# A two-layer diffusion trunk: attention recorded one block ahead, the differential maps combined on GpSimd, new durations in the order planner, a mask padded to 128 rows

## The chip, the cores and the metric

The kernel runs on one core of one Trainium2 chip. The metric is the device time of one execution in microseconds. Before the change the median of three runs is 3346.67 us (3345.6 to 3353.66).

## What is computed

Two layers of a transformer-like trunk over 1024 latent tokens and 256 context tokens of width 1024. Each layer normalises and modulates its input, projects it with one wide matrix, and gives the columns to four head groups: a state-space scan (SSD), grouped-query attention, a gated linear recurrence, and differential attention. Their outputs are concatenated, projected and added to the stream; a squared-ReLU MLP of width 4096 follows. Latent tokens attend to context and latent tokens (1280 keys), context tokens to context alone (256 keys), and the context stream is not needed after the second layer's attention.

The change concerns the two attentions. In the reference they are:

```python
def block_attention(q, k, v):
...
        s = jnp.einsum('bqgrd,bkgd->bgrqk', qblk, k, preferred_element_type=jnp.float32) * scale
        pr = jax.nn.softmax(s, axis=-1).astype(v.dtype)
        return jnp.einsum('bgrqk,bkgv->bqgrv', pr, v)
...
def diff_attention(q, k, v, lam, lam_init, subln_g):
    o1 = block_attention(q[:, :, 0::2], k[:, :, 0::2], v)
    o2 = block_attention(q[:, :, 1::2], k[:, :, 1::2], v)
    o = (o1.astype(jnp.float32) - lam * o2.astype(jnp.float32))
    o = rms_norm(o, subln_g) * (1.0 - lam_init)
```

So a differential head has two softmax maps over the same values. The kernel subtracts the second map, times a factor per query, from the first, and multiplies the result by the values once.

## The kernel before

**Recording and planning.** The program is written as a recording. Methods of `Trunk` call `Sched.op` for every group of instructions of one engine (matmuls that belong together are one operation), with the tiles it reads and writes and a cost in nanoseconds. Then `Sched.due` (line 380) runs along PE's operations in the order of recording, adds up their costs to due times, and carries these back through the dependences (less `HOP`, and `STRETCH` times the cost) to a priority for every operation. `Sched.run` (line 414) simulates the five queues PE, ACT, DVE, POOL and SP: an engine that is free takes the ready operation of highest priority whose new tiles can be had, and what it takes is emitted in that order. An operation that depends on another becomes ready at that one's end plus a gap: `LAT`, 150 ns, between two engines other than PE, 200 ns if either is PE. A tile's slot comes free `LAT` after its last use. On the chip every engine works through its own list strictly in that order and waits on semaphores, so the planner decides orders and slots, not times. Costs come from `act_cost` (line 290), `dve_cost` (line 299), `pool` (line 351) and `mm_cost` (line 366). An operation may be allowed on ACT or DVE (`copy("ANY", ...)`); the planner takes the one that it thinks will be done first. All instructions carry line 606, where they are emitted, so that the profile tells them apart by tile names.

**Slots.** `Trunk.__init__` (line 653) sets the classes: 30 wide SBUF tiles S with quotas per use (probability maps gP 4 and dP 8, transposed maps gT 5 and dT 5), 8 small tiles m (of which attention's statistics am may have 2), and the eight PSUM banks: scores in two groups of three banks (from 3 and from 0), transposes in 6 and 7, the value product in 6.

**A layer** (line 1628) runs its steps in the order of `ORDER`: recurrences, projections and SSD, then the attention groups G1D1 and G0D0, then the output projection in two halves, the norm and the MLP. In a group one grouped-query stream (G, two heads) and one differential stream (D, two heads of two maps) go side by side. Layer 0 has 10 query blocks of 128 (the last two are context blocks with 256 keys), layer 1 has 8.

**A block of a stream** is `att_block` (line 1399). Queries are loaded from DRAM for four G blocks or two D blocks at once (tile qt). For each of 2 or 4 maps: score matmuls (ks, qt; 12 per block and stream) into a PSUM tile of 1280 columns; one DVE instruction that scales them by the query's norm into P and takes the minimum for each row; one ACT exponential with the sum for each row. In a D block DVE then takes reciprocals, forms the factor per row (tile am), and combines the two maps of each head with one three-operand instruction over 1280 columns. After that come 20 transposes, four to a PSUM bank, copied to the tiles PT by ACT or DVE. Every second block multiplies the transposed maps of two blocks by the values (PT, V: 20 matmuls with 64-column weights, two instructions each) into one bank, in two operations. Every four blocks `attn_out` (line 1488) brings in the row factors (fac; in a D stream a norm as well, with a power on POOL, tiles asq and om) and stores the result. `attention` (line 1522) calls `att_block` for G and then D, block after block, so a block is recorded whole, up to the value product, before the next.

**The SSD mask.** `ssd_dt` (line 1156) writes cumulated sums as two groups of 10 rows, at rows 0 and 32, into a zeroed tile R of 42 rows; `ssd_group` (line 1190) spreads one of its rows over all partitions with a matmul against `pick`, also of 42 rows, 36 times in all.

Of the kernel before, what the change touches and what calls it, by code (L numbers as in the profile page):

```python
# [13 lines left out]
ALU = mybir.AluOpType  # L14
# [141 lines left out]
class Sched:  # L156
    LAT = 150.0
    HOP = 220.0
# [140 lines left out]
    def dve_cost(self, method, fast=False, n=None, **kw):  # L299
# [114 lines left out]
    def run(self, trace=None):  # L414
# [31 lines left out]
        table = 0  # L446
        done = 0
# [39 lines left out]
        while done < n:  # L487
# [9 lines left out]
            for e in names:  # L497
# [29 lines left out]
                progress = True  # L527
                if e == "ACT":
# [37 lines left out]
                for tl in o.tiles:  # L566
                    tl.ops_left -= 1
                    tl.end = max(tl.end, end)
                    if tl.ops_left == 0 and tl.slot is not None:
                        heapq.heappush(releases, (tl.end + self.LAT, tl.cls, tl if tl.cls == "psum" else tl.slot, tl.stream))  # L570
# [77 lines left out]
class Trunk:  # L648
# [27 lines left out]
    def setup(self):  # L676
# [7 lines left out]
        self.pick = self.const(10, "pick", dt=F32R)[0:42, :]  # L684
        s.copy("DVE", self.pick, c[0:42, 438:448])
# [470 lines left out]
    def ssd_dt(self, l, dtraw):  # L1156
# [21 lines left out]
        s.op("POOL", [("memset", dict(ap=R[0:42, 0:1024].f, constant=0.0))], 1300)  # L1178
# [11 lines left out]
    def ssd_group(self, l, g, xs, B, C, zmake):  # L1190
# [37 lines left out]
        for i, c in enumerate(order):  # L1228
# [6 lines left out]
            s.mms([dict(out=pb.v, lhsT=self.pick[:, c:c + 1].bc([42, 128]), rhs=self.acr[0:42, 512 * g:512 * g + 512],  # L1235
# [538 lines left out]
```

## Time and profile before

| | |
|---|---|
| median of the runs shown | 3346.67 us |
| the runs | 3346.67, 3353.66, 3345.6 us |
| profiled execution, first to last instruction | 3352.2 us |
| instructions | 45841 |
| mean granted TensorE clock | 0.990 |
| busy: PE, PEld, DVE, ACT, POOL | 97%, 78%, 65%, 35%, 4% |

The profiled execution has no other time of its own than this span. PE is TensorE's matmuls, PEld its weight loads, which run beside the matmuls; DVE is VectorE, ACT ScalarE, POOL GpSimd, SP the engine that issues the DMAs. A matmul is written as its weights' rows x columns and the moving operand's shape, so that 128*64 128x256 has weights of 64 columns. Matmuls overlap in their records, and a late one is a longer one, so that a busy PE need not be one at its full rate; spacing from start to start tells more.

### The profile page before, as it was taken

Reading aid. Unit: us, or ns where it says so; the run is one execution under the profiler, and the core shown is the slowest. Engines: PE = TensorE matmul, PEld = TensorE weight load, DVE = VectorE, ACT = ScalarE, POOL = GpSimd, SP = SyncE. Lnnn points to the kernel's source line nnn. Section 1 sums busy time; section 2 is a strip of 40 time slices with the busy share of each in tenths; the row PEclk is TensorE's granted clock in tenths of the full one; section 3 lists DMA queues with packets and bytes.
Section 4 is the critical chain, followed back from the end, with each engine's and each line's share of the span. In section 5 each row is a group of like instructions: output and inputs, shape, how many; then the busy total and the mean of one; then the engine's idle time right before and its main releaser. Section 6 shows DMA issues by size and latency. Waiting matters only on the chain. (4 is left out here: it accounts for less than half of the span.)

```text
span 3352.2 us, 45841 instructions
## 1 busy us (share of the span) xinstructions
PE 3258.6 (97%) x18456; PEld 2622.8 (78%) x18456; DVE 2171.1 (65%) x3785; ACT 1166.4 (35%) x2026; POOL 147.1 (4%) x168
## 2 busy tenths in 40 slices
PE   8999989999999999999999999999999999999999
PEld 6877786677688888887887888886677788888887
DVE  4787789894565555554556688689883655555554
ACT  5554447772311110101112554438771311111111
POOL 0010040000000000000000010030000000000000
PEclk9999999999999999999999989989999999999999
DMA  8443261416212222212110321151433111111111
GB/s 247 140 125 97 89 175 41 110 35 232 70 48 75 72 79 67 78 57 85 42 45 26 118 73 50 57 154 39 97 116 121 41 51 51 51 44 46 49 50 57
DMA packets 253868, 276.51 MB, mean 82 GB/s; under 512 B 22876, under 2 KB 212184, under 8 KB 253656
## 3 DMA queue, kind: packets, MB, share of 16 engines
q1 hardware_dynamic: 253656, 273.59, 27.0%
q8 instruction: 145, 2.38, 0.3%
q14 instruction: 67, 0.55, 0.1%
HBM read 218.75 MB, written 54.79 MB: 82 GB/s over the span
## 5 line engine op out<-in xcount | busy, mean ns | idle before, releaser
L606 DVE SCALAR_TENSOR_TENSOR hR<-banks,mod,hR 128x512 f32<-128x512 f32 x720 | 497.2, 697 | 420.4 <-PE banks L606 420.4
L606 PE MATMUL banks<-uh,wh 128*128 128x512 f32 (+1 forms) x1808 | 682.4, 377 | 5.8 <-ACT cvr L606 1.9
L606 PE MATMUL banks<-uh,wl 128*128 128x512 f32 (+1 forms) x1808 | 669.1, 370 | 1.7 <-DVE wl L606 1.7
L606 PE MATMUL banks<-ul,wh 128*128 128x512 f32 (+1 forms) x1808 | 669.0, 370 | 1.3 <-DVE ul L606 1.2
L606 ACT ACTIVATE wh<-wr 128x1024 fp32r<-128x1024 f32 (+2 forms) x193 | 189.5, 992 | 1050.7 <-PE banks L606 1009.9
L606 PE MATMUL banks<-hh,wh 128*128 128x512 f32 (+1 forms) x1280 | 476.7, 372 | 0.0
L606 PE MATMUL banks<-hl,wh 128*128 128x512 f32 (+1 forms) x1280 | 475.5, 371 | 0.0
L606 PE MATMUL banks<-hh,wl 128*128 128x512 f32 (+1 forms) x1280 | 474.8, 371 | 0.0
L606 PEld LDWEIGHTS banks<-uh,wh 128*128 128x128 f32 x1808 | 341.3, 189 | 98.8 <-issue 26.1
L606 PEld LDWEIGHTS banks<-uh,wl 128*128 128x128 f32 x1808 | 340.6, 188 | 65.4 <-DVE wl L606 3.0
L606 PEld LDWEIGHTS banks<-ul,wh 128*128 128x128 f32 x1808 | 341.1, 189 | 61.5 <-DVE ul L606 3.7
L606 DVE TENSOR_SCALAR_CACHE_REDUCE P<-banks,rq 128x1280 f32<-128x1280 f32 (+1 forms) x216 | 301.3, 1427 | 29.4 <-PE banks L606 28.1
L606 DVE TENSOR_TENSOR r<-r 128x512 f32<-128x512 f32 x160 | 102.2, 639 | 333.6 <-ACT r L606 331.4
L606 PEld LDWEIGHTS banks<-hh,wh 128*128 128x128 f32 x1280 | 240.8, 188 | 53.5 <-DVE hR L606 5.3
L606 ACT ACTIVATE P<-P,am 128x1280 f32<-128x1280 f32 (+1 forms) x216 | 273.4, 1272 | 21.1 <-DVE P L606 19.8
L606 PEld LDWEIGHTS banks<-hh,wl 128*128 128x128 f32 x1280 | 240.4, 188 | 44.7
L606 PEld LDWEIGHTS banks<-hl,wh 128*128 128x128 f32 x1280 | 240.6, 188 | 43.3
L606 PE MATMUL banks<-wh,uh 128*128 128x256 f32 (+2 forms) x784 | 250.4, 319 | 6.0 <-DVE qkw L606 4.2
L606 DVE TENSOR_TENSOR wl<-wr,wh 128x1024 fp32r<-128x1024 f32 (+2 forms) x204 | 230.4, 1137 | 27.6 <-ACT wh L606 26.1
L606 PE MATMUL banks<-ks,qt 128*128 128x512 f32 (+1 forms) x800 | 220.8, 387 | 20.2 <-DVE P L606 15.7
L606 PE MATMUL banks<-wl,uh 128*128 128x256 f32 (+2 forms) x784 | 226.3, 289 | 0.0
L606 PE MATMUL banks<-wh,ul 128*128 128x256 f32 (+2 forms) x784 | 225.5, 288 | 0.0
(241 smaller groups left out, 4341.0 us busy)
## 6 DMA issues: line engine op xcount, KB each, us to landing
wr<-in_w_mlp_dram SPq DMA_DIRECT2D x128, 512.0 KB
wm<-in_w_mod_dram SPq DMA_DIRECT2D x96, 512.0 KB
wr<-in_w_in_dram SPq DMA_DIRECT2D x40, 512.0 KB
ks<-dk SPq DMA_DIRECT2D x64, 160.0 KB
qt<-dq SPq DMA_DIRECT2D x72, 128.0 KB
wr<-in_w_out_dram SPq DMA_DIRECT2D x64, 128.0 KB
hd<-hT SPq DMA_DIRECT2D x8, 640.0 KB
ks<-gk SPq DMA_DIRECT2D x16, 320.0 KB
```

The source lines that it names most:

```text
L606: getattr(e, method)(**args)
```

## The change

The attention is split into three lists of units: `att_scores` (query load, score matmuls, scaling, exponential, and after the last map the factors and the combination), `att_turns` (transposes and copies) and `att_values` (value product and output). `attention` merges, for every block number, the score units of this block (of G and D in turn) with the transposes and values of the block before (first G's, then D's), by their weights; the transposes of D therefore stand in the second half of the next block's units.

In a D block the one combining DVE instruction per head becomes two on POOL: the second map times the factor, in place, and the first map plus this. The factor lies in am, which now is in use until the second multiplication.

The planner's numbers change: fixed parts of ACT and DVE instructions go up to about 160 to 205 ns and those of accumulating forms with them, gaps go down (35 ns between engines, 200 after PE, 55 before PE, slots free after 55, or 200 after PE), matmul costs are set anew, and an operation of PE whose weights have another tile shape than the one before is charged 190 ns. An operation on POOL with rate 1.0 is costed at 147 ns + 1 ns per element.

The SSD mask's R and `pick` get 128 rows; the rows added are zero.

```diff
-    LAT = 150.0
-    HOP = 220.0
+    LAT = 35.0
+    HOP = 150.0
+    DRAIN = 200.0
+    SWITCH = 190.0
...
-        return (52 if in_.t.cls == "psum" else 94) + n / 1.2 + 93 * aps + (93 if "accum_out" in kw else 0)
+        return (169 if in_.t.cls == "psum" else 205) + n / 1.2 + 90 * aps + (200 if "accum_out" in kw else 0)
...
+        elif method == "tensor_tensor_scan":
+            rate = 2.13
...
-        return 69 + rate * n + 61 * aps
+        return 157 + rate * n + 57 * aps + (83 if "accum_out" in kw else 0)
...
         if rhs.dt == F32R:
-            return 2.5 + (n / 2.4 if n >= 256 else n * 4 / 2.4)
-        return 2.5 + max(n * 4 / 2.4, 187)
+            return max(4 + n * 0.4453, 112)
+        return max(5 + n * 4 / 2.4, 216)
...
-        return self.op("PE", [("matmul", c) for c in calls], cost + 10)
+        return self.op("PE", [("matmul", c) for c in calls], cost)
...
+                if e == "PE":
+                    m = self.mode(o)
+                    if m != mode:
+                        mode = m
+                        o.cost += self.SWITCH
...
-                        gap = 0 if a == e and not o.nbytes else 200 if "PE" in (a, e) else self.LAT
+                        gap = 0 if a == e and not o.nbytes else self.DRAIN if e == "PE" else 55 if a == "PE" else self.LAT
...
-        self.pick = self.const(10, "pick", dt=F32R)[0:42, :]
-        s.copy("DVE", self.pick, c[0:42, 438:448])
+        self.pick = self.const(10, "pick", dt=F32R)
+        s.copy("DVE", self.pick.v, c[:, 438:448])
...
-        s.op("POOL", [("memset", dict(ap=R[0:42, 0:1024].f, constant=0.0))], 1300)
+        s.op("POOL", [("memset", dict(ap=R[:, 0:1024].f, constant=0.0))], 1300)
...
-            s.mms([dict(out=pb.v, lhsT=self.pick[:, c:c + 1].bc([42, 128]), rhs=self.acr[0:42, 512 * g:512 * g + 512],
+            s.mms([dict(out=pb.v, lhsT=self.pick[:, c:c + 1].bc([128, 128]), rhs=self.acr[:, 512 * g:512 * g + 512],
...
-                s.stt(P1[:, k0:NT], P2[:, k0:NT], m[:, 36 + h:37 + h], P1[:, k0:NT], ALU.mult, ALU.add)
+                s.pool("tensor_scalar", rate=1.0, out=P2[:, k0:NT], in0=P2[:, k0:NT], scalar1=m[:, 36 + h:37 + h],
+                       scalar2=None, op0=ALU.mult)
+                s.pool("tensor_tensor", out=P1[:, k0:NT], in0=P1[:, k0:NT], in1=P2[:, k0:NT], op=ALU.add)
```

The new `attention` and what it calls, cut to the units:

```python
    def att_scores(self, st, blk, nblk):
...
        w = sum(cn for _, cn in chunks) * (2 if gqa else 1) / 1280
        return [(w, lambda i=i: softmax(i)) for i in range(nsub)]
    def att_turns(self, st, blk):
...
        return [(0.75, lambda k=k, q=q: turn(k, q)) for k, q in keys]
    def att_values(self, st, blk, nblk):
...
        return [(3.0, lambda n=n: part(n)) for n in range(len(parts))]
    def attention(self, l, what):
...
        late = []
        for blk in range(nblk + 1):
            early = []
            if blk < nblk:
                runs = [self.att_scores(st, blk, nblk) for st in sts]
                for x in itertools.zip_longest(*runs):
                    early += [u for u in x if u]
            units = []
            for side in (early, late):
                total = sum(w for w, _ in side)
                at = 0.0
                for w, f in side:
                    units.append((at / total, len(units), f))
                    at += w
            for at, _, f in sorted(units, key=lambda u: u[:2]):
                yield (blk + at) / (nblk + 1)
                f()
            late = []
            if blk < nblk:
                for st in sts:
                    late += self.att_turns(st, blk)
                    if blk % 2:
                        late += self.att_values(st, blk, nblk)
```

## Rows read from the trace of the kernel before

**Rows 1.** The page's busy times: us, share of the span, instructions

```profile
PE 3258.6 (97%) x18456; PEld 2622.8 (78%) x18456; DVE 2171.1 (65%) x3785; ACT 1166.4 (35%) x2026; POOL 147.1 (4%) x168
```

**Rows 2.** Busy by stretch, in layer 1's MLP; columns as in rows 3

```profile
2800.00:2900.00 100.00, 100.00 (x433) 81.01 (x432) 53.78 (x72) 13.19 (x16) 0.00 (x0) 1.00 0.15 43
```

**Rows 3.** By stretch: length, PE, PEld, DVE, ACT, POOL busy us (x), clock, DMA, GB/s

```profile
488.00:770.00 282.00, 260.28 (x1890) 193.36 (x1889) 252.41 (x434) 219.16 (x391) 7.14 (x5) 0.99 0.27 76
...
1900.00:2250.00 350.00, 333.61 (x2147) 289.83 (x2147) 284.65 (x613) 169.57 (x344) 50.15 (x55) 0.95 0.27 79
2250.00:2515.00 265.00, 246.75 (x1749) 183.04 (x1748) 235.05 (x361) 202.53 (x336) 8.56 (x5) 0.99 0.30 86
```

**Rows 4.** PE's timeline in layer 0's attention: start us, length us, instructions

```profile
607.54 0.60 PE L606 MATMUL banks<-cst,P 128*128 128x128 f32 x4
...
609.95 4.54 PE L606 MATMUL banks<-PT,V 128*64 128x256 f32 x40
...
615.61 1.09 PE L606 MATMUL banks<-cst,fac 128*64 128x128 f32 x16
```

**Rows 5.** PE groups by form, 2250 to 2515: busy us, mean ns | idle before, releasers

```profile
L606 PE MATMUL banks<-cst,P 128*128 128x128 f32 x622 | 90.0, 279 | 9.2 <-ACT PT L606 6.0 <-DVE P L606 1.2 <-DVE PT L606 0.8
L606 PE MATMUL banks<-ks,qt 128*128 128x512 f32 x256 | 88.3, 436 | 8.2 <-DVE P L606 7.4
...
L606 PE MATMUL banks<-PT,V 128*64 128x256 f32 x600 | 68.9, 382 | 0.4 <-ACT PT L606 0.2
...
L606 PE MATMUL banks<-ks,qt 128*128 128x256 f32 x128 | 31.8, 297 | 0.0
```

**Rows 6.** PE groups by form, 488 to 770

```profile
L606 PE MATMUL banks<-cst,P 128*128 128x128 f32 x664 | 95.6, 278 | 8.4 <-ACT PT L606 5.0 <-DVE P L606 1.2 <-DVE PT L606 0.9
L606 PE MATMUL banks<-ks,qt 128*128 128x512 f32 x252 | 86.7, 438 | 10.6 <-DVE P L606 8.4 <-DMA qt<-dq 1.7
L606 PE MATMUL banks<-PT,V 128*64 128x256 f32 x656 | 75.2, 382 | 1.3 <-ACT PT L606 1.1
L606 PE MATMUL banks<-ks,qt 128*128 128x256 f32 x158 | 37.7, 299 | 0.1
```

**Rows 7.** DVE and ACT groups by form, 2250 to 2515

```profile
L606 DVE TENSOR_SCALAR_CACHE_REDUCE P<-banks,rq 128x1280 f32<-128x1280 f32 x96 | 145.4, 1546 | 11.5 <-PE banks L606 10.8
L606 ACT ACTIVATE P<-P,am 128x1280 f32<-128x1280 f32 x96 | 130.9, 1370 | 10.6 <-DVE P L606 10.0
...
L606 ACT ACTIVATE PT<-banks 128x512 f32<-128x512 f32 x123 | 68.7, 598 | 19.4 <-PE banks L606 16.4 <-issue 2.7
...
L606 DVE SCALAR_TENSOR_TENSOR P<-P,am,P 128x1280 f32<-128x1280 f32 x32 | 48.3, 1549 | 0.5
...
L606 ACT ACTIVATION_READ_ACCUMULATOR P<-P,am 128x1 f32 x96 | 19.5, 203 | 0.0
...
L606 DVE RECIPROCAL am<-am 128x4 f32<-128x4 f32 x16 | 2.8, 175 | 4.7 <-ACT P L606 4.7
```

**Rows 8.** POOL groups by form: the power (2250 to 2515), two memsets (whole span)

```profile
L606 POOL TENSOR_TENSOR om<-om,cst 128x8 f32<-128x8 f32 x3 | 4.9, 1638 | 203.6 <-DVE om L606 203.6
...
L606 POOL MEMSET bd<- 128x1024 f32 x2 | 1.9, 952 | 1.0 <-PE banks L606 1.0
L606 POOL MEMSET acr<- 42x1024 f32 x2 | 1.9, 948 | 0.0
```

**Rows 9.** PE's timeline around one of the 36 masks

```profile
2180.26 0.28 PE L606 MATMUL banks<-wl,uh 128*128 128x256 f32 x1
2180.38 0.28 PE L606 MATMUL banks<-wh,ul 128*128 128x256 f32 x1
2180.59 0.50 PE L606 MATMUL banks<-acr,pick 42*128 42x512 f32 x1
2181.01 0.39 PE L606 MATMUL banks<-wh,uh 128*128 128x256 f32 x1
```

**Rows 10.** ACT's timeline in layer 0's attention: two copies in a row

```profile
601.21 1.09 ACT L606 ACTIVATE PT<-banks 128x512 f32<-128x512 f32 x2 [0.41 <-PE banks L606]
```

More of the change, by code (lines that the diff above doesn't have):

```diff
@@ L446, in run @@
         table = 0
+        mode = None
         done = 0
@@ L1425, in att_block @@
             for c0, cn in chunks:
-                s.mms([dict(out=pb[:, c0:c0 + cn], lhsT=q, rhs=k[:, c0:c0 + cn], start=(e == 0),
+                s.mms([dict(out=pb[:, c0:c0 + cn], lhsT=qt[:, c:c + 128], rhs=k[:, c0:c0 + cn], start=(e == 0),
                             stop=(e == len(kk) - 1)) for e, k in enumerate(kk)])
@@ L1432, in att_block, with finish @@
             S.append(P)
-        fb = fac[:, 2 * blk:2 * blk + 2]
-        if gqa:
-            s.dve("reciprocal", out=fb, in_=m[:, 24:26])
-            Ps = S
-        else:
+            if i == nsub - 1:
+                finish(m)
+        def finish(m):
+            fb = st["fac"][:, 2 * blk:2 * blk + 2]
+            if gqa:
+                s.dve("reciprocal", out=fb, in_=m[:, 24:26])
+                st["P", blk] = S
+                return
             s.dve("reciprocal", out=m[:, 32:36], in_=m[:, 24:28])
@@ L1457, in turn, with part @@
                                identity=self.ident) for i, (h, j) in enumerate(srcs)])
-            s.copy("ANY", T[key][:, 0:1024].r("p (j c) -> p j c", j=4)[:, :, 128 * ab:128 * ab + 128],
+            s.copy("ANY", st["T"][key][:, 0:1024].r("p (j c) -> p j c", j=4)[:, :, 128 * ab:128 * ab + 128],
                    pt.v.r("p (j c) -> p j c", j=4))
-        if blk < 8:
-            for h in range(2):
-                for e in (0, 4):
-                    turn((h, e), [(h, e + i) for i in range(4)])
-        turn(8, [(h, j) for h in range(2) for j in (8, 9)])
-        if ab == 0:
-            return
-        b4 = blk % 4
-        if b4 == 1:
-            st["o"] = s.tile("h", 512, F32, p + "o", "ao")
-        ob = st["o"]
-        pv = s.tile("psum", 512, F32, "pv", "ppv")
-        for part in (((0,), (4, 8)) if blk < 8 else ((8,),)):
+        keys = [((h, e), [(h, e + i) for i in range(4)]) for h in range(2) for e in (0, 4)] if blk < 8 else []
+        keys.append((8, [(h, j) for h in range(2) for j in (8, 9)]))
+        return [(0.75, lambda k=k, q=q: turn(k, q)) for k, q in keys]
+    def att_values(self, st, blk, nblk):
+        s, gqa, V3 = self.s, st["gqa"], st["V"]
+        b4 = blk % 4
+        cur = {}
+        parts = ((0,), (4, 8)) if blk < 8 else ((8,),)
+        def part(n):
+            if n == 0:
+                if b4 == 1:
+                    st["o"] = s.tile("h", 512, F32, st["p"] + "o", "ao")
+                cur["pv"] = s.tile("psum", 512, F32, "pv", "ppv")
+            pv, T = cur["pv"], st["T"]
             calls = []
-            for e in part:
+            for e in parts[n]:
                 for i in range(2 if e == 8 else 4):
@@ L1482, in att_block, with attention @@
             s.mms(calls, par=1.8)
-        c = 128 * (b4 - 1)
-        s.copy("ANY", ob[:, c:c + 256], pv[:, 0:256])
-        if b4 == 3 or blk == nblk - 1:
-            self.attn_out(st, blk - b4, b4 + 1)
+            if n == len(parts) - 1:
+                c = 128 * (b4 - 1)
+                s.copy("ANY", st["o"][:, c:c + 256], pv[:, 0:256])
+                if b4 == 3 or blk == nblk - 1:
+                    self.attn_out(st, blk - b4, b4 + 1)
+        return [(3.0, lambda n=n: part(n)) for n in range(len(parts))]
+    TCLS = dict(g="S", d="S")
+    SKEW = 1
+    def attention(self, l, what):
+        nblk = 10 if l == 0 else 8
+        sts = [self.att_open(l, "gqa" if what[i] == "G" else "diff", int(what[i + 1])) for i in range(0, len(what), 2)]
+        late = []
[21 more added lines that the diff above has]
+                        late += self.att_values(st, blk, nblk)
     def attn_out(self, st, b0, nb):
@@ L1520, in attn_out @@
             s.dma(d[:, 128 * b0:128 * b0 + n], v.f)
-    def attention(self, l, what):
-        nblk = 10 if l == 0 else 8
-        sts = [self.att_open(l, "gqa" if what[i] == "G" else "diff", int(what[i + 1])) for i in range(0, len(what), 2)]
-        for blk in range(nblk):
-            for i, st in enumerate(sts):
-                yield (blk + i / len(sts)) / nblk
-                self.att_block(st, blk, nblk)
     def out_proj(self, l, gis, ks):
```

54 lines of the change are left out of this document (32 added, 22 removed).

## The prediction

> **What bounds the kernel now.** First the page: TensorE is busy for 97% of the 3352.2 us span [rows 1]. A busy PE row counts matmuls that overlap or crawl, so the second view asks what the same matmuls cost where nothing disturbs them. In a stretch of the second layer's MLP, 433 matmuls of 512 columns take 100 us, 0.231 us each, and PEld, the weight loads, is busy 81% [rows 2]. The stages come third: in the two attention stretches, 488 to 770 and 2250 to 2515, PEld falls to 69% while DVE stands at 90% and 89% and ACT at 78% and 76% [rows 3]. That is where time can be found.
>
> How much: price each PE instruction of a stretch at its undisturbed spacing. A 512-column score costs 0.231 us, a 256-column one half of that, 0.1155. Four transposes in a row take 0.60 us, of which the last one's own length is 0.28, so (0.60 - 0.28) / 3 = 0.11 each; 40 value matmuls take 4.54, 0.1135 each [rows 4, 5]. For 2250 to 2515 the counts are 256, 128, 622 and 600 [rows 5]: 59.1 + 14.8 + 68.4 + 68.1 = 210.4 us. The other 143 matmuls of the stretch (1749 in all) are mostly the output step at 1.09 / 16 = 0.068 and a few at 0.1 to 0.23; at 0.1 they make 14.3. So 225 us of work stand in 265: **40 us lost**. For 488 to 770, with 252, 158, 664 and 656 [rows 6] and 160 others: 58.2 + 18.2 + 73.0 + 74.5 + 16 = 240 of 282: **42 us lost**.
>
> Who causes it: PE's plain idle time before the score matmuls waits for DVE P, 7.4 us of 8.2, that before the transposes for ACT PT, 6.0 of 9.2 [rows 5]; the rest of the loss is hidden in matmuls that start late. The chain of one block is scores, the DVE pass of 1.546 us, the exponential of 1.370, in a D block the DVE combination of 1.549 per head, then transposes and their copies [rows 7]. All of it is recorded for one block before the next begins.
>
> **The change, part by part.**
>
> *Combination on GpSimd.* DVE loses 32 instructions of 1549 ns in layer 1's stretch, 48.3 us [rows 7], and as many full ones in layer 0. DVE there falls from 235.1 to 187 us, with ACT at 202.5 [rows 3]; PSUM copies may run on either, so both can settle near 195. PE's 225 us are then the longest by 30.
>
> GpSimd gains four passes per D block, over 1280 elements each. No row shows such a pass. The nearest is its memset of 1024 elements in 952 ns [rows 8], 1.19 us for 1280. Lower end: every pass at that, 4.8 us per block. Upper end: one memset time per stream touched, two for the multiplication (2.4), three for the sum (3.6), 11.9 per block. I take one per input, 1.2 + 2.4 per head, 7.1 per block, between the ends and nearer to the only row. A full step, a G and a D block, is PE work of 2 x (8 x 0.231 + 4 x 0.1155 + 20 x 0.11 + 4.54 / 2) = 13.6 us plus about 1 of output step, 14.6. So GpSimd is not the bound even at 11.9. Its latency is covered because the D transposes are now recorded from about the middle of the following step, some 7 us after the maps' last exponential; the cover is other PE work: the next block's scores and the G block's transposes.
>
> The Trainium skill's GPSIMD Engine Reference, Elementwise side-by-side cycle accounting, gives 4497 ns for a two-input add of 2048 elements, an estimate of 2.8 us for 1280. With that in place of 2.4 the block takes 7.9 us and the sum stays; no run here shows it yet.
>
> *Queued behind it.* The power for the output step, 1638 ns in the second layer [rows 8], stands in POOL's queue behind up to one block's passes, 7.1 us (4.8 to 11.9). Ten such steps exist; VectorE's scaling and PE's small broadcast matmuls wait for it. The next use of their tile is two blocks away, so I cost it at nothing; without that cover it is at most 10 x 7.1 = 71 us, and PE would show it in front of the om matmuls.
>
> *Recording one block ahead.* Scores of block n+1 are interleaved with transposes and values of block n. Nothing is added, but the values come in two parts that other work may separate: 32 parts in layer 1. Going to another tile shape and back costs PE time: the matmul ahead of the 42-row mask takes 0.21 instead of 0.12 us to the next start, the mask 0.42 instead of 0.23 [rows 2, 9]: 0.09 in and 0.19 out. So 32 x 0.28 = 9 us stay lost in layer 1 and 10 in layer 0 with its 36. Two group starts per layer, each with its own first loads, keep about 2 us each. That leaves 40 - 13 = 27 and 42 - 14 = 28, 55 us as the best case for attention. I take four fifths, **44 us**: with DVE and ACT at 195 / 250 = 78% they can still be late, as in 1900 to 2250, where DVE at 81% goes with PE at 95% and a clock of 0.95 [rows 3]. Lower end: 0, if another wait takes the place (rivals). The query loads stay on SP ahead of the first scores of their pair, the same number, past no other queue.
>
> *Mask padded.* 36 masks lose up to 0.28 us each, 10 us. They sit where PE often waits for VectorE's wk and ACT's exponentials; half, **5 us**. Filling 128 rows instead of 42 costs POOL nothing: 948 ns for 42 rows against 952 for 128 [rows 8].
>
> *Planner.* No instruction changes, only orders and slots, everywhere. A pair of ACT copies takes 1.09 us and one 0.598 [rows 7, 10], so the second starts 0.49 after the first. The old formula's 52 + 427 = 479 ns is that spacing; the new 169 + 427 = 596 is the length. With the new numbers the planner thinks ACT and DVE fuller than they are, and hands work over sooner (35 instead of 150 ns). The two nearly cancel along a chain. I take 0, from -20 to +20: the whole loss in 1900 to 2250 is PE's idle 16 us plus slow matmuls, and an order can mend or double it.
>
> **Sum:** 44 + 5 + 0 = 49 us off the profiled execution's span of 3352.2, the only time of its own that is shown: 3303. That span lies 5.5 above the median of the runs, 3346.67, so **3298 us**. Own range of this case: attention 25 to 55, mask 0 to 10, planner 20 either way: 3262 to 3335.
>
> **Rivals.**
>
> 1. *The maps come late (slower).* The planner prices a GpSimd pass at 147 + 1280 ns = 1.43, 5.7 us per block. At the upper end of 11.9 the last map lands 6.2 us after the planned moment, and PE, strictly in order, stands at its transposes. If half of that lands on PE, 32 D blocks x 3.1 = 99 us against the 49 won: 3397. From 1.5 us per D block on (49 / 32) it is slower than before. For it: the price has no row and the planner's is below my middle. Against: the half step of cover. Chance 0.12.
>
> 2. *The statistics tile becomes the wait (no change).* Only two of the small tiles am exist for both streams, and a D block's is now held until GpSimd has read it in the second multiplication. Filling one takes four DVE passes, an exponential, its readout and the reciprocal, 4 x 1.55 + 1.37 + 0.2 + 0.2 = 8.0 us [rows 7]; at 1.2 + 2.4 + 1.2 = 4.8 for GpSimd the turn is 12.8, under the step's 14.6. At the upper end, 2.4 + 3.6 + 2.4 = 8.4, it is 16.4, as long as a step today: layer 1 has two head groups of eight blocks, 16 steps in 265 us, 16.6 each. Then only mask and planner are left: 3342. Against: the G block's tile comes free earlier. Chance 0.08.
>
> 3. *The relief is not one (no change).* If a GpSimd pass and a DVE instruction with two operands in SBUF exclude each other, DVE loses waiting what it won. Those left in the stretch are one small am instruction in each of 16 D blocks and a few per output step; taken as 40, with waits of half a 2.4 us pass, they are 48 us, the 48.3 saved. Then the 44 us of attention fall away: 3342. No row shows POOL reading large tiles beside DVE. The Trainium skill's Perfetto Trace Analysis, Optimizing Scalar/DVE Operations, says that offloading between those two "might not help" because of a shared read port. Against: the DVE passes read PSUM and one scalar, and the small ones of a D block come just ahead of its GpSimd work. Chance 0.08.
>
> 4. *The planner finds more.* Better orders in the projections, 20 us, with all 55 and the mask's 10: 3262 and below. Chance 0.10.
>
> **How the numbers follow.** Forecast 0.62, rivals 0.12, 0.08, 0.08, 0.10. A measurement here can tell about 0.3%, 10 us, from no change. Forecast and rival 4 are faster by more, and a third of rivals 2 and 3 too: 0.77. Within 10 us lies the rest of these two: 0.11. Slower: 0.12. The range runs from 3260, which leaves out half of rival 4, to 3343, which takes in 2 and 3 and leaves out 1: about 0.17 outside.
>
> **What would show it.** Right: DVE P without the three-operand instruction, POOL near 7 us per D block, the attention stretches about 22 us shorter each, PE waits for DVE P and ACT PT below 5 us, mask matmuls followed after 0.23 us. Rival 1: PE waits for POOL P. Rival 2: DVE's first pass of a D block waits for POOL. Rival 3: small DVE instructions that last microseconds. The prediction is wrong in its core if the stretches keep their 282 and 265 us.

## The result and the profile after

The changed kernel takes 3490.73 us (median of four runs, 3486.15 to 3493.97) beside 3350.16 us for the kernel before (four runs, 3345.6 to 3358.3): a ratio of 1.041, 95% interval 1.0387 to 1.0432. It is slower by 140 us, where 49 us less were forecast. Its profiled execution spans 3492.1 us. Two medians below include one execution far above the others of its kernel (3783.27 us where the planner is told GpSimd's price, 10818.06 where it gets the gaps alone); without it they would be 3481.69 and 3391.64, and the ratios leave it out.

The page's busy times, which answer to [rows 1]:

```profile
PE 3301.9 (95%) x18456; PEld 2659.1 (76%) x18456; DVE 2106.6 (60%) x3638; ACT 1216.2 (35%) x2101; POOL 576.8 (17%) x312
```

DVE lost 64 us of work, POOL took on 430, and TensorE, with the same 18456 matmuls, is busy for 43 us more. Where the time went shows in one table by stage. The bounds are read from TensorE's timeline: the first score matmul and the first matmul of the output projection of each layer, and the end of the first layer's MLP. So the rows are the set-up with the first layer's projections, its attention, the rest of that layer, the second layer's projections, its attention, and the rest. The kernel before, by stretch (length, busy us and count of each engine, granted clock, DMA share, GB/s):

```profile
0.00:485.00 485.00, 458.27 (x3140) 380.98 (x3141) 356.31 (x788) 235.71 (x471) 64.95 (x85) 0.98 0.49 147
485.00:769.00 284.00, 260.97 (x1892) 193.48 (x1890) 253.92 (x437) 219.30 (x392) 9.57 (x6) 0.99 0.27 76
769.00:1845.00 1076.00, 1073.73 (x5595) 868.21 (x5595) 573.24 (x942) 169.61 (x252) 7.70 (x13) 1.00 0.23 72
1845.00:2250.00 405.00, 388.61 (x2427) 334.11 (x2426) 312.65 (x661) 191.17 (x379) 52.69 (x57) 0.95 0.30 90
2250.00:2503.00 253.00, 234.75 (x1664) 174.06 (x1663) 228.77 (x352) 195.64 (x324) 8.56 (x5) 0.99 0.28 77
2503.00:3352.00 849.00, 842.26 (x3748) 671.96 (x3746) 446.20 (x609) 154.98 (x212) 3.65 (x3) 1.00 0.19 59
```

The changed kernel, the same stages:

```profile
0.00:512.00 512.00, 466.75 (x3141) 388.69 (x3142) 364.31 (x798) 236.13 (x466) 64.06 (x86) 0.96 0.46 139
512.00:856.00 344.00, 282.50 (x1892) 208.16 (x1893) 233.72 (x402) 222.50 (x383) 223.30 (x81) 0.91 0.22 59
856.00:1934.00 1078.00, 1074.79 (x5606) 869.70 (x5605) 555.79 (x889) 194.24 (x308) 9.93 (x16) 1.00 0.23 73
1934.00:2350.00 416.00, 386.21 (x2415) 333.65 (x2414) 310.60 (x654) 192.61 (x380) 58.12 (x57) 0.94 0.27 82
2350.00:2641.00 291.00, 247.06 (x1649) 185.17 (x1648) 211.23 (x325) 201.01 (x320) 204.88 (x66) 0.92 0.26 70
2641.00:3492.00 851.00, 844.63 (x3763) 673.69 (x3761) 430.94 (x576) 169.71 (x246) 16.46 (x7) 1.00 0.19 60
```

The two attentions grow by 60 and 38 us, but the set-up grows too, by 27, and the second layer's projections by 11, where neither the recording of attention nor GpSimd has a part. The first attention has 1892 matmuls in both kernels. Its 60 us are 38.5 of plain idle time (344 - 282.5 against 284 - 261) and 21.5 of a longer busy time for the same matmuls, with a mean granted clock of 0.91 instead of 0.99. Of the forecast's 22 us less per attention nothing is there.

GpSimd's groups by form over the whole span of the changed kernel (busy us, mean ns, idle before), the operation that [rows 8] did not have:

```profile
L623 POOL TENSOR_SCALAR P<-P,am 128x1280 f32<-128x1280 f32 x64 | 226.3, 3542 | 172.0 <-DVE fac L623 92.3 <-DVE am L623 31.2 <-PE banks L623 16.9
L623 POOL TENSOR_TENSOR P<-P,P 128x1280 f32<-128x1280 f32 x64 | 187.9, 2957 | 0.0
```

A head takes 3.54 + 2.96 = 6.5 us and a D block 13.0, above the upper end of 11.9 that the prediction had drawn. What TensorE waited for in the changed kernel (us, times, longest):

```profile
PE banks L623 <- DVE P L623: 48.4, 47, 5.2
PE banks L623 <- DVE PT L623: 16.8, 17, 6.0
PE banks L623 <- ACT PT L623: 15.7, 23, 4.2
...
PE banks L623 <- POOL P L623: 8.2, 3, 5.6
PE banks L623 <- DVE om L623: 7.0, 4, 4.3
```

GpSimd is named for 8.2 us only. Its lateness also reaches TensorE through VectorE, as two places of the changed kernel's timeline show (start us, length us, engine, instructions, idle before and its releaser):

```profile
621.77 7.02 POOL L623 TENSOR_SCALAR P<-P,am 128x1280 f32<-128x1280 f32 x2 [6.91 <-DVE fac L623]
...
628.77 1.67 POOL L623 TENSOR_TENSOR om<-om,cst 128x8 f32<-128x8 f32 x1
...
630.47 2.83 DVE L623 TENSOR_TENSOR om<-om,fac 128x8 f32<-128x8 f32 x1 [2.67 <-POOL om L623]
633.36 1.98 PE L623 MATMUL banks<-cst,om 128*64 128x128 f32 x16 [4.32 <-DVE om L623]
...
2463.30 6.41 POOL L623 TENSOR_TENSOR P<-P,P 128x1280 f32<-128x1280 f32 x2
2463.64 3.27 DVE L623 TENSOR_TENSOR mo<-ao,mo 128x512 fp32r<-128x512 f32 x1
...
2466.83 1.54 DVE L623 TENSOR_SCALAR_CACHE_REDUCE P<-banks,rq 128x1280 f32<-128x1280 f32 x1
...
2468.43 0.86 PE L623 MATMUL banks<-ks,qt 128*128 128x512 f32 x3 [3.63 <-DVE P L623]
```

In the first, the power of the output step stands behind two multiplications on POOL; VectorE's scaling of om comes late and takes 2.83 us for eight columns beside the next sums, and TensorE stands for 4.32 us. In the second, a small VectorE subtraction, with both operands in SBUF, lasts 3.27 us beside GpSimd's sums; the pass that empties the score banks is queued behind it, and TensorE waits 3.63 us for "DVE P". How long such VectorE instructions last by form, first in the kernel before, then in the changed one:

```profile
L606 DVE TENSOR_TENSOR mo<-ao,mo 128x512 fp32r<-128x512 f32 x16 | 11.0, 686 | 0.2
L606 DVE CAST mo<-ao 128x512 fp32r<-128x512 f32 x13 | 5.5, 427 | 0.4
```

```profile
L623 DVE TENSOR_SCALAR_CACHE_REDUCE P<-banks,rq 128x1280 f32<-128x1280 f32 x192 | 291.7, 1547 | 102.3 <-PE banks L623 79.0 <-POOL P L623 21.0 <-issue 2.0
...
L623 DVE TENSOR_TENSOR mo<-ao,mo 128x512 fp32r<-128x512 f32 x16 | 33.5, 2095 | 1.8 <-ACT mo L623 1.4
L623 DVE CAST mo<-ao 128x512 fp32r<-128x512 f32 x9 | 13.9, 1545 | 0.1
```

The large pass, which reads PSUM, keeps its 1547 ns (1546 in [rows 7]); the subtraction and the cast became three and three and a half times as long, on average.

### The profile page after: what moved, and what is told of

Its sections match the earlier page's. It is cut to its first block, busy times and chain, and to the rows that moved or that the text cites. A ratio compares the mean times of both kernels' runs of the same rounds, so it can differ in the third digit from the quotient of the medians.

```text
span 3492.1 us, 46113 instructions
## 1 busy us (share of the span) xinstructions
PE 3301.9 (95%) x18456; PEld 2659.1 (76%) x18456; DVE 2106.6 (60%) x3638; ACT 1216.2 (35%) x2101; POOL 576.8 (17%) x312
## 5 line engine op out<-in xcount | busy, mean ns | idle before, releaser
L623 ACT ACTIVATE wh<-wr 128x1024 fp32r<-128x1024 f32 (+2 forms) x158 | 151.2, 971 | 959.5 <-PE banks L623 745.2
L623 PE MATMUL banks<-ks,qt 128*128 128x512 f32 (+1 forms) x800 | 231.3, 411 | 59.4 <-DVE P L623 48.4
L623 POOL TENSOR_SCALAR P<-P,am 128x1280 f32<-128x1280 f32 (+1 forms) x72 | 234.0, 3257 | 185.8 <-DVE fac L623 99.5
L623 PE MATMUL banks<-cst,P 128*128 128x128 f32 x1312 | 204.6, 290 | 41.2 <-DVE PT L623 15.8
```

What stands on the lines that cost most here:

```text
L623: getattr(e, method)(**args)
```

## The experiments

All medians stand beside runs of the kernel before on the same chip, 3351.9 to 3354.8 us in every group.

**One part at a time.** First the changed kernel with the combination back on VectorE:

```diff
-                s.pool("tensor_scalar", rate=1.0, out=P2[:, k0:NT], in0=P2[:, k0:NT], scalar1=m[:, 36 + h:37 + h],
-                       scalar2=None, op0=ALU.mult)
-                s.pool("tensor_tensor", out=P1[:, k0:NT], in0=P1[:, k0:NT], in1=P2[:, k0:NT], op=ALU.add)
+                s.stt(P1[:, k0:NT], P2[:, k0:NT], m[:, 36 + h:37 + h], P1[:, k0:NT], ALU.mult, ALU.add)
```

> The changed kernel with the combination of the two maps back on DVE, one three-operand instruction per head; recording one block ahead, planner and mask stay as changed. Theory GPSIMD (its passes of 3.54 and 2.96 us, 13 us per D block, are late, and DVE's mo instructions wait behind them): the two attention stretches lose what they lost before the change or less, some 100 us come back of the 140, about 3385 us. Theory PLANNER (the new durations make worse orders everywhere): 3440 or more, since the planner is untouched. Theory RECORDING (one block ahead runs out of slots or statistics tiles): 3440 or more, since the order of recording is untouched.

Measured: 3411.27 us, ratio 1.0179 [1.0164, 1.0194]. GpSimd is worth 79 us of the loss; 58 us remain without it. That lies between the forecasts of the theories: GpSimd is the largest part, but not 100 us. TensorE's two waits for VectorE are far shorter here than in the list above, where they are 48.4 and 16.8:

```profile
PE banks L623 <- DVE P L623: 20.4, 42, 1.3
...
PE banks L623 <- DVE PT L623: 3.9, 7, 0.9
```

So with the combination on GpSimd these two grow by 41 us, and the wait for "POOL P" by 8.2: by name, most of GpSimd's lateness arrives through VectorE.

The kernel before with that edit the other way round, the two GpSimd instructions in place of `s.stt`:

> The kernel before with nothing but the combination moved to GpSimd, in the old order of recording and with the old planner. Theory GPSIMD: clearly slower than before; each of 32 full D blocks has 13 us of GpSimd where 3.1 us of DVE stood, with no block recorded in between to cover them; if half of the 9.9 more lands on the end, 32 x 5 = 160 us, about 3500. Theories PLANNER and RECORDING: DVE is relieved and the rest is as before, within 30 us of 3350.

Measured: 3444.34 us, 1.0271 [1.0254, 1.0289], 91 us more than the kernel before and between the forecasts. TensorE waits there 28.0 us in 26 places for "POOL P".

The kernel before with the planner's new numbers (every line of the diff in `Sched`) and nothing else:

> The kernel before with nothing but the planner's new numbers (durations, gaps, shape charge). Theory PLANNER: about 140 us slower, 3490. Theory GPSIMD, in which the planner has only the 36 us that are lost outside the attention stretches: about 3386. If the numbers were good in themselves: 3350 or less.

Measured: 3446.85 us, 1.0281 [1.026, 1.0302]: 94 us, from orders and slots alone, between the forecasts. Its set-up, both attentions and the projections between them, by stretch:

```profile
0.00:512.00 512.00, 467.33 (x3141) 386.43 (x3142) 363.55 (x798) 237.21 (x467) 65.63 (x86) 0.97 0.47 140
512.00:819.00 307.00, 271.13 (x1895) 202.71 (x1896) 249.62 (x433) 224.75 (x392) 6.38 (x5) 0.96 0.23 64
...
1899.00:2313.00 414.00, 387.12 (x2412) 331.36 (x2410) 311.19 (x654) 192.18 (x381) 60.91 (x58) 0.94 0.28 86
2313.00:2586.00 273.00, 240.41 (x1659) 176.72 (x1660) 225.16 (x346) 202.34 (x330) 8.18 (x5) 0.97 0.26 74
```

Every stage in which several engines feed each other is longer than before, by 27, 23, 9 and 20 us; the set-up and the projections are as long as in the changed kernel, to 2 us.

The changed kernel with the planner's old numbers, the same lines turned back:

> The changed kernel with the old planner numbers (a GpSimd pass still costed at 147 ns + 1 ns per element). Theory PLANNER: back to about 3350 or better. Theory GPSIMD: the 100 us of the attention stretches stay and only the some 36 us outside come back, about 3455. Theory RECORDING: as GPSIMD, 3455.

Measured: 3448.75 us, 1.0291 [1.0276, 1.0306], so within the change the planner is worth 42 us, near to what the theory of GpSimd foretold. Here the lateness of the maps is named as such in TensorE's waits:

```profile
PE banks L606 <- POOL P L606: 31.6, 11, 5.7
```

Old numbers and the combination on VectorE, so that recording ahead and the padded mask are left:

> The changed kernel with the combination on DVE and the old planner numbers: what is left of the change is the recording one block ahead and the padded mask. So far the planner's numbers alone cost 94 us and GpSimd alone 92, and the change 138 in all, so the rest must win. If the parts simply add: 3353 - (94 + 92 - 138) = 3305. If recording ahead helps only where the planner or GpSimd makes the work late: within 15 us of 3353 less the mask's 10, about 3343.

Measured: 3364.16 us, 1.0031 [1.0021, 1.0042], above both forecasts. Beside the run above, 3448.75, it prices GpSimd at 85 us under the old numbers. Its two attentions:

```profile
484.00:782.00 298.00, 267.37 (x1898) 196.98 (x1897) 244.50 (x422) 231.21 (x411) 8.77 (x6) 0.98 0.24 67
...
2253.00:2513.00 260.00, 235.35 (x1668) 173.80 (x1669) 221.41 (x340) 205.13 (x339) 8.55 (x5) 0.99 0.28 77
```

Recording ahead does not shorten them: 298 and 260 us against 284 and 253 before.

The kernel before with the padded mask alone:

```diff
-        self.pick = self.const(10, "pick", dt=F32R)[0:42, :]
+        self.pick = self.const(10, "pick", dt=F32R)
...
-        s.op("POOL", [("memset", dict(ap=R[0:42, 0:1024].f, constant=0.0))], 1300)
+        s.op("POOL", [("memset", dict(ap=R[:, 0:1024].f, constant=0.0))], 1300)
```

> The kernel before with nothing but the 128-row mask. The old planner prices a matmul by its columns alone, so the orders stay the same. 36 masks at up to 0.28 us: 3353 - 10 = 3343 if PE is the last to arrive in the scan, 3353 if it waits for DVE and ACT there anyway.

Measured: 3338.87 us, 0.9957 [0.9941, 0.9973], faster than both kernels. The set-up and the second layer's projections, the two stages with 18 masks each, take 8 and 10 us less, the attentions the same 284 and 253:

```profile
0.00:477.00 477.00, 450.43 (x3142) 379.33 (x3142) 355.85 (x789) 236.22 (x472) 66.04 (x85) 0.99 0.49 150
...
1836.00:2231.00 395.00, 377.09 (x2419) 326.88 (x2418) 310.96 (x658) 190.53 (x378) 52.69 (x57) 0.97 0.31 91
```

TensorE's timeline around a mask, to be read beside [rows 9]:

```profile
2155.64 0.39 PE L606 MATMUL banks<-acr,pick 128*128 128x512 f32 x1
2155.87 0.28 PE L606 MATMUL banks<-wh,uh 128*128 128x256 f32 x1
```

The next matmul starts 0.23 us after the mask, where it was 0.42: this sign of the prediction came.

These runs lie on a path from one kernel to the other: 3353.0 before (the middle of its groups), 3338.9 with the padding, 3364.2 with recording ahead, 3411.3 with the planner's numbers, 3490.7 with GpSimd. The steps are -14, +25, +47 and +79. They are not parts that add in any order: the planner costs 94 alone and 42 to 47 here.

**What of GpSimd costs.** The changed kernel with attention's last cast moved to ScalarE and the subtraction to GpSimd, which takes most of the stretched VectorE instructions away (the scalings of om remain):

```diff
-        s.copy("ANY", hi, o[:, 0:n])
-        s.tt(lo, o[:, 0:n], hi.f, ALU.subtract)
+        s.copy("ACT", hi, o[:, 0:n])
+        s.pool("tensor_tensor", rate=2.2, out=lo, in0=o[:, 0:n], in1=hi.f, op=ALU.subtract)
```

> The changed kernel with the last step of the attention output, the split into a high and a low part (mo), taken from DVE: the cast to ACT, the subtraction to POOL. In the changed kernel these DVE instructions take 2.1 and 1.5 us instead of 0.7 and 0.4. If they are held by GpSimd's passes (two SBUF operands of DVE against GpSimd's reads), no long DVE instruction is left in the attention stretches, DVE wins 33 us there, PE's 6 us stops behind them go, and the kernel is 10 to 40 us faster than the changed one: 3450 to 3480. If the time is lost through GpSimd's lateness alone: 3480 to 3500.

Measured: 3492.62 us, 1.0416 [1.0396, 1.0435], no change. GpSimd has 20.8 us more to do (16 subtractions of 1301 ns) and TensorE's wait for "POOL P" rises from 8.2 to 12.6 us, while that for "DVE P" falls from 48.4 to 42.9 only. VectorE's large pass now waits longer for "POOL P", 31.7 instead of 21.0 us:

```profile
L623 DVE TENSOR_SCALAR_CACHE_REDUCE P<-banks,rq 128x1280 f32<-128x1280 f32 x192 | 292.2, 1547 | 130.2 <-PE banks L623 93.4 <-POOL P L623 31.7 <-DMA mixl<-mo 2.8
```

So the stretched instructions were one way by which the lateness arrived, and without them it arrives by others.

The changed kernel with the planner told what a GpSimd pass takes:

```diff
-                s.pool("tensor_scalar", rate=1.0, out=P2[:, k0:NT], in0=P2[:, k0:NT], scalar1=m[:, 36 + h:37 + h],
+                s.pool("tensor_scalar", rate=2.65, out=P2[:, k0:NT], in0=P2[:, k0:NT], scalar1=m[:, 36 + h:37 + h],
...
-                s.pool("tensor_tensor", out=P1[:, k0:NT], in0=P1[:, k0:NT], in1=P2[:, k0:NT], op=ALU.add)
+                s.pool("tensor_tensor", rate=2.2, out=P1[:, k0:NT], in0=P1[:, k0:NT], in1=P2[:, k0:NT], op=ALU.add)
```

> The changed kernel with the planner told what the trace shows for GpSimd's passes: 3.54 us for the multiplication, 2.96 for the sum, instead of 1.43 each. If the wrong price is what hurts (PE sent to transposes that are not ready): most of GpSimd's 79 us come back, 3420. If the passes hurt by their length and by holding DVE: 3470 to 3500.

Measured: 3482.47 us, 1.0384 [1.0362, 1.0406]. Of 79 us, 8 come back, no more than a mere shift of the planner's numbers can move the time (below, up to 10): the price was wrong, but a right one mends little.

The changed kernel with half the length on GpSimd; the other half of the second map is left out of the result:

```diff
-                s.pool("tensor_scalar", rate=1.0, out=P2[:, k0:NT], in0=P2[:, k0:NT], scalar1=m[:, 36 + h:37 + h],
+                kh = (k0 + NT) // 2
+                s.pool("tensor_scalar", rate=1.0, out=P2[:, k0:kh], in0=P2[:, k0:kh], scalar1=m[:, 36 + h:37 + h],
...
-                s.pool("tensor_tensor", out=P1[:, k0:NT], in0=P1[:, k0:NT], in1=P2[:, k0:NT], op=ALU.add)
+                s.pool("tensor_tensor", out=P1[:, k0:kh], in0=P1[:, k0:kh], in1=P2[:, k0:kh], op=ALU.add)
```

> The changed kernel with GpSimd working on half of the columns (the other half of the second map is left out of the result), so 6.5 instead of 13 us per D block, and the planner's price halved with it. If GpSimd costs by its length (maps late, tiles held): more than half of its 79 us come back, 3411 to 3445. If it costs by having another engine and its queue in the chain at all: 3460 or more.

Measured: 3420.84 us, 1.0208 [1.0192, 1.0223]. TensorE's wait for "DVE P" is down to 22.9 us. The GpSimd groups:

```profile
L623 POOL TENSOR_SCALAR P<-P,am 128x640 f32<-128x640 f32 x64 | 120.9, 1899 | 287.3 <-DVE fac L623 119.1 <-ACT PT L623 66.1 <-PE banks L623 49.8
L623 POOL TENSOR_TENSOR P<-P,P 128x640 f32<-128x640 f32 x64 | 98.3, 1556 | 0.7
```

A D block takes 2 x (1.90 + 1.56) = 6.9 us on GpSimd and costs 10 us in all (3420.8 against 3411.3), where 13.0 us cost 79. The cost does not go with the length. That it begins where the passes outlast the work beside them fits these two points; no length between them was run. The run also bears on the relief of VectorE. The two attentions of the kernel with the combination on VectorE, then those of this run:

```profile
513.00:817.00 304.00, 272.73 (x1891) 198.75 (x1891) 246.16 (x422) 228.95 (x400) 6.43 (x5) 0.97 0.24 67
...
2311.00:2563.00 252.00, 233.65 (x1670) 174.07 (x1670) 221.53 (x339) 206.26 (x336) 10.19 (x6) 1.00 0.31 84
```

```profile
515.00:820.00 305.00, 270.40 (x1894) 199.44 (x1895) 205.93 (x401) 224.33 (x394) 124.37 (x85) 0.96 0.24 67
2313.00:2573.00 260.00, 234.52 (x1662) 175.61 (x1662) 187.73 (x324) 199.42 (x319) 112.11 (x66) 0.98 0.29 81
```

VectorE does 206 and 188 us of work instead of 246 and 222, and the attentions take 305 and 260 us against 304 and 252.

The changed kernel with four statistics tiles instead of two:

```diff
-        s.cls("m", sb, 8, 48, dict(ln=3, att=2, qk=4, ssd=2))
+        s.cls("m", sb, 10, 48, dict(ln=3, att=4, qk=4, ssd=2))
```

> The changed kernel with four statistics tiles am for attention instead of two (ten small tiles instead of eight). If the wait for the statistics tile is what GpSimd's 13 us cost (rival 2 of the prediction): DVE's waits for POOL P go and 30 to 79 us come back, 3411 to 3460. If the late maps are: 3475 to 3505.

Measured: 3467.12 us, 1.035 [1.0332, 1.0367], 24 us better than the changed kernel and between the two forecasts. VectorE's idle time before its large pass for "POOL P" falls from 21.0 us (above) to 16.8, TensorE's wait for "DVE P" from 48.4 to 36.5, and TensorE's for "POOL P" rises from 8.2 to 24.4. What VectorE waits for there can be seen in the changed kernel's timeline:

```profile
554.79 5.73 POOL L623 TENSOR_TENSOR P<-P,P 128x1280 f32<-128x1280 f32 x2
...
557.70 1.55 DVE L623 TENSOR_SCALAR_CACHE_REDUCE P<-banks,rq 128x1280 f32<-128x1280 f32 x1 [4.20 <-POOL P L623]
```

The pass starts as the first of the two sums ends, half of 5.73 us after 554.79. A sum reads two maps and no longer am, so this wait is for a map's tile. The other waits of the large pass for "POOL P" that stand by themselves in the timeline end with a sum as well. Whether the 24 us come from am or from the other order that the planner makes with more tiles is not shown; more tiles for the maps were not tried.

The kernel before, padded, with one of two heads on GpSimd, priced at the lengths measured:

```diff
-                s.stt(P1[:, k0:NT], P2[:, k0:NT], m[:, 36 + h:37 + h], P1[:, k0:NT], ALU.mult, ALU.add)
+                if h == 0:
+                    s.stt(P1[:, k0:NT], P2[:, k0:NT], m[:, 36 + h:37 + h], P1[:, k0:NT], ALU.mult, ALU.add)
+                else:
+                    s.pool("tensor_scalar", rate=2.65, out=P2[:, k0:NT], in0=P2[:, k0:NT], scalar1=m[:, 36 + h:37 + h],
+                           scalar2=None, op0=ALU.mult)
...
```

> The kernel before with the 128-row mask and the combination of one head of the two on GpSimd, costed by its traced length. If GpSimd's length is covered up to some 6.5 us per block: DVE's relief of 1.5 us per D block shows and the time is 3339 or up to 25 us less. If the order drawn decides: 3339 to 3400.

Measured: 3426.6 us, 1.0223 [1.0208, 1.0239], 88 us more than the padded kernel and outside both forecasts. Its groups by form:

```profile
L606 POOL TENSOR_SCALAR P<-P,am 128x1280 f32<-128x1280 f32 x32 | 142.4, 4449 | 302.5 <-DVE am L606 128.5 <-PE banks L606 74.2 <-ACT PT L606 71.4
...
L606 DVE SCALAR_TENSOR_TENSOR P<-P,am,P 128x1280 f32<-128x1280 f32 x32 | 58.6, 1833 | 0.8
```

Now VectorE's combination and GpSimd's multiplication are released by the same factors and run side by side: 1833 ns instead of 1549 [rows 7], and 4449 instead of 3542. Half the GpSimd work costs as much as all of it did, where a block is recorded whole.

**What of the planner costs.** The kernel before with a third of the new numbers at a time: the lines of `act_cost` and `dve_cost`; the gaps and releases (`LAT`, `HOP`, `DRAIN`); the matmul costs with `SWITCH`.

> The kernel before with nothing but the new durations of ACT and DVE instructions (fixed parts, accumulators, scans). Theory LENGTH (the new numbers are lengths from the trace, while an engine starts the next instruction before the last has ended, so that the planner takes ACT and DVE for fuller than they are): most of the planner's 94 us, 3420 or more. Theory GAPS (the shorter gaps send work to PE before it is ready): 3340 to 3370.

> The kernel before with nothing but the new gaps and slot releases (35 instead of 150 ns between engines, 55 instead of 200 before PE, slots free after 55). Theory GAPS: 3420 or more. Theory LENGTH: 3340 to 3370.

> The kernel before with nothing but the new PE costs: matmuls by their measured spacing and 190 ns for a change of tile shape. Both theories: within 15 us of 3353, since these costs are nearer to what the trace shows. If any other set of numbers than the old one makes worse orders, because the old order is a lucky one: 3380 or more here too.

Measured: 3421.01 us, 1.0207 [1.0192, 1.0222] for the durations; 3393.15, 1.0117 [1.01, 1.0134] for the gaps; 3396.26, 1.0128 [1.0108, 1.0147] for the matmul costs. No third is to blame alone: 69, 40 and 44 us, where all three give 94. The theory that record lengths mislead the planner foretold the first, but not the other two (3340 to 3370, and within 15 us of 3353). For the matmul costs the reading that any set other than the old one makes worse orders had foretold 3380 or more, and that came.

Neighbours of the old set (`LAT` 155 and `HOP` 225; then `cost + 12` for `cost + 10`) and of the new one (`LAT` 40, `HOP` 155) tell whether an order is luck:

> The kernel before with LAT 155 instead of 150 and HOP 225 instead of 220, numbers that are no better or worse than the old ones. Theory PICKED (the old order is the best of many that were tried, and any shift of the numbers draws another one): 20 to 60 us slower, 3373 to 3413. Theory WRONG NUMBERS (orders drawn from sound numbers are about equal): within 12 us of 3352.

> The kernel before with every PE operation costed 2 ns higher (10 to 12). As for the run with the shifted gaps: PICKED 3373 to 3413, WRONG NUMBERS within 12 us of 3352.

> The kernel before with the planner's new numbers, but LAT 40 instead of 35 and HOP 155 instead of 150; no instruction is added or taken away. Theory: the new numbers as a set mislead the planner, so a neighbouring set gives about the same: 3425 to 3470 us, against 3447 with the exact set and 3353 for the kernel before. Rival: 3447 is one bad order out of a wide scatter, and another draw may lie anywhere; then it comes under 3400 or over 3490. Two neighbours of the old set gave 3363 and 3353.

Measured: 3363.19 us, 1.0032 [1.0022, 1.0042]; 3353.29, 1.0005 [0.9996, 1.0014]; 3445.31, 1.0276 [1.0259, 1.0293]. Such a shift moves the time by up to 10 us in these three; the new set stays at 3445 when it is moved. So the 94 us belong to the numbers and not to one unlucky order. Whether the old numbers are nearer to the chip, or only fitted to this kernel in a wider neighbourhood than these small shifts reach, stays open.

The padding under the neighbour with `cost + 12`:

> The kernel before with the mask of 128 rows, and the cost of a group of matmuls +12 instead of +10. Theory: the padding takes away tile shape switches and is worth its 10 to 15 us under any neighbouring order: 3335 to 3346 us against 3353 for the same numbers without padding. Rival: the 14 us were partly a better order that the padding brought about by chance, and with a neighbouring order less than 5 of them are left: 3348 to 3363 us.

Measured: 3343.0 us, 0.9968 [0.9959, 0.9978]: 10 us under the same numbers without it, 3353.29.

## Why the prediction was wrong

**The loss in attention and its cause.** That TensorE loses some 40 us in each attention was worked out from spacings; no run here won any of it back, so how much of it can be had is open. That the order of recording was the cause does not stand: with nothing but recording ahead and the mask, TensorE's attentions are 14 and 7 us longer, and the step measures 25 us of loss where 44 of gain were taken, below its lower end of 0. Under the new planner's numbers it is a gain: 3446.9 to 3411.3 is 36 us, of which the mask accounts for 10 to 14. I read a wait in front of the transposes as one that another recording would fill; but the recording only sets due times, and the planner makes its own order from them. That this is why nothing was gained is argued, not shown. The 44 us rested on VectorE's relief as well; what that brings is under rival 3.

**GpSimd's price.** Taken 7.1 us per D block between 4.8 and 11.9, measured 13.0. The upper end failed on the multiplication, which I bounded by two memset times, 2.4 us: it takes 3.54. The sum, 2.96, lay inside its 3.6. The estimate worked out from the Trainium skill's GPSIMD Engine Reference, Elementwise — side-by-side cycle accounting, 2.8, was near to that.

**"Its latency is covered."** The cover was put at some 7 us. With 6.9 us of GpSimd work the loss is 10 us, with 13.0 it is 79: a cover of that size fits, and the price went past it. So the outcome of rival 1 came (chance 0.12): the maps come late, at 79 / 32 = 2.5 us per D block, past its limit of 1.5. Its path came only in part. It had TensorE stand at the transposes because the planner's price is too low; with the measured price 71 of the 79 us stay, and its sign, the wait for "POOL P", is 8.2 us beside 41 more for "DVE P" and "DVE PT". That its 99 us stand near 79 is partly luck. How the 79 us divide between late maps, held VectorE instructions and tiles that come free late is not shown.

**"Queued behind it", costed at nothing.** The timeline shows the queue at work, and TensorE waits 7.0 us for om, the sign that was named. It is small, but the cover named, two blocks until the tile's next use, did not hold: TensorE's own broadcast needs the result at once.

**Rival 2, the statistics tile.** Open. With the lengths measured, its own sum makes the turn 8.0 + 10.0 = 18.0 us, longer than a step of 16.6, and two more tiles return 24 us. But the waits of VectorE that were its sign end with a sum, so they are for a map's tile and not for am.

**Rival 3, the relief is not one.** Its mechanism is there; its price was not. Subtractions with two operands in SBUF and casts last 2.1 and 1.5 us on average in the changed kernel, 3.27 us in the row above, and the three-operand combination is held as well in the run with one head. The Trainium skill, SBUF — State Buffer, Who interferes with whom, says that a VectorE instruction with two SBUF inputs contends with a GpSimd instruction that reads SBUF, that a cast can contend too, and that the one issued first keeps the shared ports for its whole instruction; the rows agree, with the pass that reads PSUM at its old 1547 ns. But moving the small ones away gained nothing. Nor did the relief itself show: with half the passes on GpSimd, VectorE has 40 and 34 us less to do and the attentions are no shorter. That VectorE's 90% was not the bound fits this; a gain that GpSimd's remaining 6.9 us per block eat up is not excluded.

**The planner, taken as 0 from -20 to +20.** Measured +94 alone, +42 to +47 within the change. I had seen that the new durations are the records' lengths where the old ones were spacings (0.598 against 0.49 us for a copy [rows 7, 10]) and let it cancel against the shorter gaps along a chain. It does not: the durations alone cost 69 us and the shorter gaps alone 40, with the same sign. The Trainium skill's Perfetto Trace Analysis, Optimizing Scalar/DVE Operations, gives some 51 and 93 ns as ScalarE's overhead of an instruction and says that the profiled latency is about twice that, as its second half overlaps with the next instruction; the old formula's 52 and 94 are these, and the spacing of the trace agrees. Why the new matmul costs hurt, though 4 + 512 x 0.4453 = 232 ns is just the undisturbed spacing of [rows 2], is not settled; nor is by which order each stage loses. They are nearer to spacings and lose 44 us, so lengths in place of spacings cannot be the whole cause. Shown is only that the loss comes with the numbers and not with one draw of them.

**The mask.** 36 x 0.28 = 10 us was the upper end; I halved it because TensorE often waits beside the masks. Measured 14 and, under the neighbouring numbers, 10: all of it arrived, in the two stages that have masks. The mechanism was right, and the term was mis-sized by that half.

**The sum.** It added 44 + 5 + 0, with nothing for GpSimd, and took the parts as independent, while what each is worth depends on the numbers by which it is planned. Three steps were wrong in the same direction: attention's recording by 69 us (-44 taken, +25 measured), the planner by 47, GpSimd by 79; the mask gave back 9. The upper end of the case's own range, 3335, was mis-added too: 25 + 0 - 20 leave 5 us off, 3342.

## What to carry to other kernels

Before an elementwise pass is moved to another engine, its latency is to be set against the work that really stands between its producer and its consumer: here 6.9 us per D block were nearly free where another block's work was recorded beside them and 13.0 cost 79, while 7.5 us cost 88 in the run with one head, where a block is recorded whole. Any new set of a planner's costs is a change of its own, to be timed by itself with a neighbour or two beside it: costs nearer to what the trace shows were no better here. The plainest edit was the one that paid: the kernel before with the mask padded to 128 rows takes 3338.87 us, and no other version here is faster.

## What the runs showed of the hardware

GpSimd's multiplication of a map by one factor per row is slower than its sum of two maps: 3542 against 2957 ns for 1280 columns, 1899 against 1556 for 640. Neither was to be guessed from its memset, 952 ns for 1024 columns [rows 8].

In the changed kernel's attention TensorE also has less clock where it stops again and again. Of these two stretches, columns as in the tables by stage, the first has no stop and the second has several, the 4.32 us shown above as the last:

```profile
600.00:616.00 16.00, 16.00 (x131) 10.82 (x130) 11.89 (x17) 9.04 (x15) 12.84 (x4) 1.00 0.05 17
...
622.00:633.00 11.00, 4.63 (x23) 3.21 (x22) 6.74 (x6) 3.84 (x6) 11.00 (x4) 0.55 0.00 0
```

Busy for the whole of 16 us, TensorE had 1.00 of its upper level, 2.4 GHz; busy for 4.63 of 11 us it had 0.55, near its lower level, 1.2 GHz. The 16 small matmuls that follow take 1.98 us, where as many took 1.09 in the kernel before [rows 4]. Over that attention the mean is 0.91 instead of 0.99, and the same 1892 matmuls were busy for 282.5 us instead of 261.0, a third of that stage's loss. An estimate from the two clocks, 261.0 x 0.99 / 0.91 = 284, puts most of this third down to the clock.
